# Placing a decoder trunk's matmul operands at 128-byte and 512-byte boundaries of their SBUF partition

## The chip, the core and the metric

One core of a Trainium2 chip runs the whole kernel as one program. The metric is the device time of one execution in microseconds; several executions are timed and their median is given. One more execution runs under the hardware profiler, and all rows below are from that one.

## What is computed

The reference is a two-layer decoder trunk on 256 tokens of width 1024, in float32. Layer 0 is a half-weighted SwiGLU feed-forward, a Mamba-2 mixer and another feed-forward; layer 1 is a feed-forward, sliding-window attention over shared keys and values, and another feed-forward; a norm ends it. Cut to what matters here:

```
swiglu(h) = (silu(h @ w_gate) * (h @ w_up)) @ w_down      # 1024 -> 2816 -> 1024, four times
x = x + 0.5 * swiglu(rmsnorm(x))                          # layer 0, first
x = x + mamba2_mixer(rmsnorm(x))                          # w_in, conv, scan in chunks of 128, w_out
x = x + 0.5 * swiglu(rmsnorm(x))                          # layer 0, second
k, v = shared_kv(x)                                       # one K and one V projection
x = x + 0.5 * swiglu(rmsnorm(x))                          # layer 1, first
x = x + swa_sink_attention(rmsnorm(x), k, v)              # w_q, softmax with sinks, w_o
x = x + 0.5 * swiglu(rmsnorm(x))                          # layer 1, second
return rmsnorm(x)
```

## The kernel before

**Units.** All weights are cut into 341 units of 128 x 1024 numbers, listed in `ORDER`; a unit feeds a product with a contraction of 1024 (gate, up, and the projections) or with 1024 outputs (down, the two output projections). Activations lie transposed: a tile holds 128 features on the partitions and the 256 tokens along the free axis.

**Parts.** To keep float32 accuracy with the fast one-pass type (`F32R`), each number is split in two parts, high and low, and a product takes three of the four combinations: high x high, high x low, low x high. For a weight unit, `Weights.high` (L144, ScalarE) rounds the raw weights to the tile `hi`, and `Weights.low` (L155, VectorE) subtracts to get `lo`; both are 128 x 1024, from pools of six buffers each. The raw weights come by DMA, two units (1 MB) at a time, into four buffers `raw`. `Weights.ahead` keeps the split four units ahead of the matmuls.

**The three ways in which a unit is multiplied**, each with 6144 columns streamed through TensorE per unit:

- `wide` (L359), for gate and up: the moving operand's two parts lie side by side in one tile `xs` (512 columns: `xh`, then `xl`). Per 128-column slice of the unit, `hi` is loaded and all 512 columns streamed, then `lo` is loaded and the first 256 streamed: 16 loads and 16 matmuls. In two of the four feed-forwards (`by_part`, where the layer number differs from the index in the layer) the eight `hi` slices come first, then the eight `lo` slices; in the other two they alternate.
- `unit` (L346), for the mixer's projections `sb`, for `q`, and for the keys `kab`: three matmuls of 256 columns per slice, 24 loads and 24 matmuls. `sb` and `q` take the moving parts from `xs`; `kab` takes them from tiles of its own, `xkh` and `xkl`.
- `rows` (L379), for down (`da`), the mixer's output (`sa`) and the attention's output (`aa`): also 24 loads and 24 matmuls of 256 columns, with moving parts in `hh`/`hl`, `yh`/`yl`, `oh`/`ol`.

TensorE follows `ORDER` by hand: gate, up, and four steps behind, down. Small steps on the other engines are put between units by `Slots`.

**Places.** A tile's address within its partition comes from the order of allocation. Without a request, tiles begin at multiples of 32 bytes. These are the places that the built programs give, as the remainder of the first byte by 128 and by 512. A weight slice is 512 bytes of a partition, a moving part 1024.

| tile | before: mod 128 | before: mod 512 | changed: mod 128 | changed: mod 512 |
|---|---|---|---|---|
| `hi`, `lo` (all six buffers, every slice) | 32 | 160 | 0 | 0 |
| `xs` (gate, up, `sb`, `q`) | 0 | 128 | 0 | 128, 256, 384, 0, 0, 128, 256, 384 |
| `hh` / `hl` (down) | 32 | 160 | 0 | 384 / 0 |
| `yh` / `yl` (mixer's output) | 32 | 416 | 0 | 128 / 256 |
| `oh` / `ol` (attention's output) | 32 | 416 | 0 | 128 / 256 |
| `xkh`, `xkl` (keys, values) | 32 | 160 | 0 | all four multiples of 128 |
| `raw` | 32 | 160 | 32 | 416 |

For the value product (`v`) the parts change roles: `xkh` and `xkl` are loaded and `hi` and `lo` are streamed.

Of the kernel before, what the change touches and what calls it, by code (L numbers as in the profile page):

```python
# [10 lines left out]
F32R = mybir.dt.float32r  # L11
# [5 lines left out]
P = 128  # L17
T = 256
D = 1024
KT = D // P  # L20
NF = 2816 // P
LAG = 4
SLACK = 2

NORM_AT = (1, 0, 0, 0)
SCALE_AT = (0, 0, 1, 0)
# [83 lines left out]
class Weights:  # L110
# [27 lines left out]
    def high(self, half=None):  # L138
        u = self.rounded
        c, i = divmod(u, CH)  # L140
        if not half:
            self.hi = self.parts.tile([P, D], F32R, tag="hi", name=f"hi{u}")
        hi, s = self.hi, self.piece(half)
        self.nc.scalar.activation(hi[:, s], self.chunks[c][:, i, s], AF.Copy)  # L144
        if half != 0:
            self.ready[u] = hi
            self.rounded += 1

    def low(self, half=None):
        u = self.cut  # L150
        c, i = divmod(u, CH)
        if not half:
            self.lo = self.parts.tile([P, D], F32R, tag="lo", name=f"lo{u}")
        hi, lo, s = self.ready.get(u, self.hi), self.lo, self.piece(half)
        self.nc.vector.tensor_tensor(lo[:, s], self.chunks[c][:, i, s], hi[:, s].bitcast(F32), ALU.subtract)  # L155
        if half == 0:
            return
        self.ready[u] = (hi, lo)
        self.cut += 1
        if i == CH - 1 or u == NU - 1:  # L160
            del self.chunks[c]
            self.load()
# [53 lines left out]
class Trunk:  # L216
    def __init__(self, ctx, tc, a):
        self.ctx, self.tc, self.nc, self.a = ctx, tc, tc.nc, a
        nc = self.nc
        self.NPART = 6  # L220
        cp = self.cp = ctx.enter_context(tc.tile_pool(name="const", bufs=1))
        self.wk = ctx.enter_context(tc.tile_pool(name="work", bufs=2))
        raw = ctx.enter_context(tc.tile_pool(name="raw", bufs=RAW))
        parts = ctx.enter_context(tc.tile_pool(name="parts", bufs=self.NPART))
        self.ps = ctx.enter_context(tc.tile_pool(name="ps", bufs=4, space=PSUM))
        self.W = Weights(nc, a["w"], raw, parts)

        self.sm = cp.tile([P, NSM], F32, name="sm")
        self.co = cp.tile([P, NCO], F32, name="co")
        xp = [cp.tile([P, 2, T], F32, name=f"X{k}") for k in range(KT // 2)]  # L230
        self.X = [xp[k // 2][:, k % 2] for k in range(KT)]

        self.xs = [cp.tile([P, 2 * T], F32R, name=f"xs{k}") for k in range(KT)]
        self.xh = [x[:, 0:T] for x in self.xs]
        self.xl = [x[:, T:] for x in self.xs]
        self.ones = cp.tile([P, P], F32, name="ones")
        nc.vector.memset(self.ones, 1.0)
        self.mhalf = cp.tile([P, 2], F32, name="mhalf")
        nc.gpsimd.memset(self.mhalf, -0.5)
        self.eps = cp.tile([P, 1], F32, name="eps")  # L240
        nc.gpsimd.memset(self.eps, EPS)
        warm = cp.tile([P, 1], F32, name="warm")
        nc.scalar.activation(warm, self.ones[:, 0:1], AF.Silu)

        def first(t):
            q, h = nc.sync.dma_start, D // 2
            q(self.norms, a["norms"])
            q(xp[0], a["x"][:, 0:2, :])
            q(t[:, 0, :h], a["w"][0, :, 0, :h])
            q(xp[1], a["x"][:, 2:4, :])  # L250
            q(xp[2], a["x"][:, 4:6, :])
            q(t[:, 0, h:], a["w"][0, :, 0, h:])
            q(xp[3], a["x"][:, 6:8, :])
            for i in range(1, CH):
                q(t[:, i, :], a["w"][0, :, i, :])

        self.norms = cp.tile([P, NNO], F32, name="norms")
        self.W.load(first)
        self.W.load()
        nc.sync.dma_start(self.co, a["const"])  # L260
        self.W.load()
        nc.sync.dma_start(self.sm, a["small"])
        for _ in range(RAW - 3):
            self.W.load()
        self.ident = self.cc("ident")
        self.slots = Slots()
# [207 lines left out]
    def ffn(self, l, i, key, nxt):  # L474
        nc, wk = self.nc, self.fw
        self.stage_norm(key)
        accs = self.accs(f"da_{key}")
        hs = {}

        def evac(f, g, u):  # L480
            hh = wk.tile([P, T], F32R, tag="hh", bufs=LAG + 2, name=f"hh_{key}_{f}")
            hl = wk.tile([P, T], F32R, tag="hl", bufs=LAG + 2, name=f"hl_{key}_{f}")
            hs[f] = (hh, hl)

            def e0():
                nc.vector.tensor_tensor(g, g, self.rs, ALU.mult)
                nc.scalar.activation(g, g, AF.Silu)
                nc.vector.tensor_tensor(u, u, self.rs, ALU.mult)

            def e1():  # L490
                nc.vector.tensor_tensor(u, u, g, ALU.mult)
                nc.scalar.activation(hh, u, AF.Copy)

            def e2():
                nc.vector.tensor_tensor(hl, u, hh.bitcast(F32), ALU.subtract)

            wait = max(0, 4 - f) if key == "f0" else 2 if f == 0 else 0
            self.slots.chain(wait, [e0, e1, e2])

        def product(name, f, t):  # L500

            b = self.bank(f"{name}_{key}_{f}")
            if self.W.pos == 0:
                self.slots.at(0, lambda: nc.scalar.copy(t, b[:, 0:T]))
                self.unit((name, l, i, f), b[:, 0:T])
                return

            def add():
                nc.scalar.copy(t, b[:, T:])  # L509
                nc.vector.tensor_tensor(t, b[:, 0:T], t, ALU.add)  # L510

            self.slots.at(0, add)
            self.wide((name, l, i, f), b, by_part=l != i and f > 0)

        for f in range(NF):
            g, u = (wk.tile([P, T], F32, tag=n, bufs=4, name=f"{n}s_{key}_{f}") for n in "gu")
            product("g", f, g)
            evac_now = lambda: evac(f, g, u)
            self.slots.late(0, evac_now)
            product("u", f, u)  # L520
            if l == 1 and i == 0 and f == 0:
                self.split_k()
            if l == 1 and i == 0 and f == 5:
                self.shared_k()
            if f >= LAG:
                self.down(l, i, f - LAG, hs, accs)
        for f in range(NF - LAG, NF - 2):
            self.down(l, i, f, hs, accs)
        self.tail([(("d", l, i, f), *hs.pop(f)) for f in (NF - 2, NF - 1)], accs, nxt)
# [15 lines left out]
    def ssm(self, nxt):  # L545
        nc, tc, wk, sl = self.nc, self.tc, self.sw, self.slots
# [17 lines left out]
        B, C, xs, zs, CSB, CB, xdt, ys, M = ({} for _ in range(9))  # L564
        yh, yl, sq, R = {}, {}, {}, {}
# [188 lines left out]
        def ysplit(tt):  # L754
            y = ys[tt]
            w = self.s("snw", tt)
            h = yh[tt] = wk.tile([P, T], F32R, tag="yh", bufs=6, name=f"yh{tt}")
            l = yl[tt] = wk.tile([P, T], F32R, tag="yl", bufs=6, name=f"yl{tt}")
            sl.at(0, lambda: A.activation(h, y, AF.Copy, scale=w))
            sl.at(1, lambda: V.scalar_tensor_tensor(l, y, w, h.bitcast(F32), ALU.mult, ALU.subtract))  # L760

# [58 lines left out]
        for what in seq[:-2]:  # L820
            if what[0] == "so":
                tt = what[1]
# [39 lines left out]

    def split_k(self):
        wk = self.kp
        self.xkh = [wk.tile([P, T], F32R, name=f"xkh{k}") for k in range(KT)]
        self.xkl = [wk.tile([P, T], F32R, name=f"xkl{k}") for k in range(KT)]
        for k in range(KT):
            w = self.nw("kvn", k)
            self.slots.at(2 + k, lambda k=k, w=w: self.nc.scalar.activation(self.xkh[k], self.X[k], AF.Copy, scale=w))
            self.slots.at(  # L870
                3 + k,
                lambda k=k, w=w: self.nc.vector.scalar_tensor_tensor(
                    self.xkl[k], self.X[k], w, self.xkh[k].bitcast(F32), ALU.mult, ALU.subtract
                ),
            )
# [26 lines left out]
    def att(self, nxt):  # L902
        nc, wk, sl = self.nc, self.aw, self.slots
        V, A = nc.vector, nc.scalar
        self.stage_norm("att")
        Q, S, SM_, PT, oh, ol = ({} for _ in range(6))
# [94 lines left out]
        def pv(j):  # L1001
# [8 lines left out]
                nc.tensor.matmul(o[:, P:T], self.V[:, 1, v], p[:, 2], start=False, stop=True, skip_group_check=True)  # L1010
            for r in range(2):
                o = bs[r * (not one)][:, r * one * T : r * one * T + T]
                h = oh[j, r] = wk.tile([P, T], F32R, tag="oh", bufs=4, name=f"oh{j}_{r}")
                ol[j, r] = wk.tile([P, T], F32R, tag="ol", bufs=4, name=f"ol{j}_{r}")
                A.activation(h, o, AF.Copy)
            for r in range(2):
                o = bs[r * (not one)][:, r * one * T : r * one * T + T]
# [214 lines left out]
```

## Time and profile before

| | us |
|---|---|
| median of 3 runs (1061.9 to 1063.26) | 1062.36 |
| the profiled execution | 1063.96 |
| its span, from the first to the last instruction | 1062.2 |
| TensorE busy (matmuls) | 1040.4 |
| VectorE busy | 775.3 |
| ScalarE busy | 627.5 |

The profiled execution's own time is 1.8 us over its span, and 1.6 us over the median. Matmuls overlap in TensorE's pipeline, so the "mean ns of one" of a matmul (283 ns for 256 columns) is not what it costs; the distance from one matmul's start to the next is. The chain of waits gives that distance: it merges a unit's matmuls in one piece, with the time until the next piece starts.

### The profile page before, as it was taken

Reading aid. Unit: us, or ns where it says so; the run is one execution under the profiler, and the core shown is the slowest. Engines: PE = TensorE matmul, PEld = TensorE weight load, DVE = VectorE, ACT = ScalarE, POOL = GpSimd, SP = SyncE. Lnnn points to the kernel's source line nnn. Section 1 sums busy time; section 2 is a strip of 40 time slices with the busy share of each in tenths; the row PEclk is TensorE's granted clock in tenths of the full one; section 3 lists DMA queues with packets and bytes.
Section 4 is the critical chain, followed back from the end, with each engine's and each line's share of the span. In section 5 each row is a group of like instructions: output and inputs, shape, how many; then the busy total and the mean of one; then the engine's idle time right before and its main releaser. Section 6 shows DMA issues by size and latency. Waiting matters only on the chain.

```text
span 1062.2 us, 18342 instructions
## 1 busy us (share of the span) xinstructions
PE 1040.4 (98%) x7290; PEld 961.3 (90%) x7290; DVE 775.3 (73%) x1420; ACT 627.5 (59%) x1106; POOL 79.5 (7%) x122
## 2 busy tenths in 40 slices
PE   8999999999999999999999999999999999999996
PEld 7899999999989898999999899999998898999996
DVE  4866666788999967766667796666689777666664
ACT  6555555579886756555555664555565765555554
POOL 3000000210111112000000200000022020000000
PEclk9999999999999999999999999999999999999998
DMA  8555455447545454545555465455544334545521
GB/s 303 202 186 198 165 197 185 174 176 273 182 149 211 160 180 165 193 168 196 188 192 189 148 216 187 170 194 192 197 170 160 110 145 173 198 172 193 191 100 40
DMA packets 30132, 190.84 MB, mean 180 GB/s; under 512 B 3904, under 2 KB 5728, under 8 KB 8544
## 3 DMA queue, kind: packets, MB, share of 16 engines
q1 hardware_dynamic: 30048, 189.69, 50.0%
q8 instruction: 57, 0.93, 0.4%
q14 instruction: 27, 0.22, 0.1%
HBM read 187.27 MB, written 1.10 MB: 177 GB/s over the span
## 4 chain that ended last, share of the span: by engine, by line
PE 81%; DVE 10%; ACT 4%; DMA 2%; POOL 1%; issue 1%; SPq 0%; ACTq 0%; DVEq 0%; POOLq 0%
PE da_f L379 23%; PE u_f L359 23%; PE g_f L359 22%; PE sa L379 4%; PE sb L346 3%; DVE lo L155 2%; PE aa L379 2%; PE q L346 1%; DMA csb<-cs_scratch 1%; DVE xs L598 1%; DVE xs L391 1%; ACT hi L144 1%; DVE E L720 1%; ACT E L715 1%; DMA raw<-w 1%
## 5 line engine op out<-in xcount | busy, mean ns | idle before, releaser
L155 DVE TENSOR_TENSOR lo<-raw,hi 128x1024 fp32r<-128x1024 f32 (+1 forms) x343 | 415.0, 1213 | 15.8 <-ACT hi L144 15.6
L144 ACT ACTIVATE hi<-raw 128x1024 fp32r<-128x1024 f32 (+1 forms) x343 | 357.4, 1047 | 22.3 <-PE da_f L379 6.2
L359 PE MATMUL u_f<-xs,hi 128*128 128x512 f32 x704 | 218.6, 398 | 0.0
L359 PE MATMUL g_f<-xs,hi 128*128 128x512 f32 x696 | 214.7, 397 | 0.6 <-DVE xs L391 0.4
L379 PE MATMUL da_f<-hh_f,hi 128*128 128x256 f32 x704 | 199.1, 283 | 0.0
L379 PE MATMUL da_f<-hl_f,hi 128*128 128x256 f32 x704 | 199.1, 283 | 0.0
L379 PE MATMUL da_f<-hh_f,lo 128*128 128x256 f32 x704 | 198.9, 283 | 0.0
L359 PEld LDWEIGHTS u_f<-xs,hi 128*128 128x128 f32 x704 | 129.8, 188 | 27.9
L359 PEld LDWEIGHTS g_f<-xs,hi 128*128 128x128 f32 x696 | 128.2, 189 | 27.4 <-DVE xs L391 1.5
L359 PE MATMUL u_f<-xs,lo 128*128 128x256 f32 x704 | 150.2, 281 | 0.0
L359 PE MATMUL g_f<-xs,lo 128*128 128x256 f32 x696 | 147.8, 281 | 0.0
L379 PEld LDWEIGHTS da_f<-hh_f,hi 128*128 128x128 f32 x704 | 134.5, 191 | 1.6
L379 PEld LDWEIGHTS da_f<-hh_f,lo 128*128 128x128 f32 x704 | 134.9, 192 | 0.0
L379 PEld LDWEIGHTS da_f<-hl_f,hi 128*128 128x128 f32 x704 | 134.8, 192 | 0.0
L510 DVE TENSOR_TENSOR gs_f<-g_f,gs_f 128x256 f32<-128x256 f32 x87 | 36.9, 424 | 121.9 <-ACT gs_f L509 121.9
L359 PEld LDWEIGHTS u_f<-xs,lo 128*128 128x128 f32 x704 | 116.0, 189 | 3.9
L359 PEld LDWEIGHTS g_f<-xs,lo 128*128 128x128 f32 x696 | 114.3, 189 | 3.8
L346 PE MATMUL sb<-xs,hi 128*128 128x256 f32 x656 | 107.8, 284 | 0.0
L510 DVE TENSOR_TENSOR us_f<-u_f,us_f 128x256 f32<-128x256 f32 x88 | 37.3, 423 | 91.1 <-ACT us_f L509 91.0
L509 ACT COPY us_f<-u_f 128x256 f32<-128x256 f32 x88 | 32.6, 371 | 113.1 <-PE u_f L359 113.1
L346 PEld LDWEIGHTS sb<-xs,hi 128*128 128x128 f32 x656 | 93.4, 188 | 1.1 <-issue 0.5
L509 ACT COPY gs_f<-g_f 128x256 f32<-128x256 f32 x87 | 32.1, 369 | 97.3 <-PE g_f L359 97.3
(252 smaller groups left out, 1376.7 us busy)
## 6 DMA issues: line engine op xcount, KB each, us to landing
raw<-w SPq DMA_DIRECT2D x168, 1024.0 KB, 4.9
csb<-cs_scratch SPq DMA_DIRECT2D x8, 768.0 KB, 7.0
raw<-w SPq DMA_DIRECT2D x4, 512.0 KB, 7.9
X<-x SPq DMA_DIRECT2D x4, 256.0 KB, 5.7
Q<-r_q SPq DMA_DIRECT2D x32, 32.0 KB, 1.9
out<-o SPq DMA_DIRECT2D x3, 256.0 KB, 2.2
ca<-const_att SPq DMA_DIRECT2D x1, 704.0 KB, 4.1
raw<-w SPq DMA_DIRECT2D x2, 256.0 KB, 5.7
```

The lines of the kernel that those rows point to most:

```text
L144: self.nc.scalar.activation(hi[:, s], self.chunks[c][:, i, s], AF.Copy)
L155: self.nc.vector.tensor_tensor(lo[:, s], self.chunks[c][:, i, s], hi[:, s].bitcast(F32), ALU.subtract)
L346: nc.tensor.matmul(out, w[:, k * P : (k + 1) * P], x[k], start=n == 0, stop=n == len(passes) - 1)
L359: self.nc.tensor.matmul(out[:, 0:c], w[:, k * P : (k + 1) * P], x[k], start=n == 0, stop=n == len(passes) - 1, skip_group_check=True,)
L379: nc.tensor.matmul(out, w[:, s], x, start=f and j < 4 and m == 0, stop=e and m == 2, skip_group_check=True)
L391: nc.vector.scalar_tensor_tensor(self.xl[j], self.X[j], wcol(j), self.xh[j].bitcast(F32), ALU.mult, ALU.subtract)
L509: nc.scalar.copy(t, b[:, T:])
L510: nc.vector.tensor_tensor(t, b[:, 0:T], t, ALU.add)
L598: V.scalar_tensor_tensor(out, u[:, tap : tap + T], self.s("convw", tap * 24 + c), out, ALU.mult, ALU.add)
L715: A.activation(e, e, AF.Exp, scale=-1.0)
L720: V.tensor_tensor(f, f, c, ALU.mult)
```

## The change

Eleven tile allocations get a wish for alignment: the two weight parts at multiples of 512 bytes, all moving parts at multiples of 128. Nothing else is edited. On every engine the instructions, their operands, their order and their waits are the same; only addresses differ, those of tiles that were allocated later too.

```diff
+BLOCK = 128
...
-            self.hi = self.parts.tile([P, D], F32R, tag="hi", name=f"hi{u}")
+            self.hi = self.parts.tile([P, D], F32R, align_bytes=4 * BLOCK, tag="hi", name=f"hi{u}")
...
-            self.lo = self.parts.tile([P, D], F32R, tag="lo", name=f"lo{u}")
+            self.lo = self.parts.tile([P, D], F32R, align_bytes=4 * BLOCK, tag="lo", name=f"lo{u}")
...
-        self.xs = [cp.tile([P, 2 * T], F32R, name=f"xs{k}") for k in range(KT)]
+        self.xs = [cp.tile([P, 2 * T], F32R, align_bytes=BLOCK, name=f"xs{k}") for k in range(KT)]
...
-            hh = wk.tile([P, T], F32R, tag="hh", bufs=LAG + 2, name=f"hh_{key}_{f}")
-            hl = wk.tile([P, T], F32R, tag="hl", bufs=LAG + 2, name=f"hl_{key}_{f}")
+            hh = wk.tile([P, T], F32R, align_bytes=BLOCK, tag="hh", bufs=LAG + 2, name=f"hh_{key}_{f}")
+            hl = wk.tile([P, T], F32R, align_bytes=BLOCK, tag="hl", bufs=LAG + 2, name=f"hl_{key}_{f}")
...
-        self.xkh = [wk.tile([P, T], F32R, name=f"xkh{k}") for k in range(KT)]
-        self.xkl = [wk.tile([P, T], F32R, name=f"xkl{k}") for k in range(KT)]
+        self.xkh = [wk.tile([P, T], F32R, align_bytes=BLOCK, name=f"xkh{k}") for k in range(KT)]
+        self.xkl = [wk.tile([P, T], F32R, align_bytes=BLOCK, name=f"xkl{k}") for k in range(KT)]
```

The tiles `yh`, `yl`, `oh` and `ol` get `align_bytes=BLOCK` in the same way.

## Rows read from the trace of the kernel before

**Rows 1.** The page, busy time by engine, and TensorE's granted clock in 40 slices.
```profile
PE 1040.4 (98%) x7290; PEld 961.3 (90%) x7290; DVE 775.3 (73%) x1420; ACT 627.5 (59%) x1106; POOL 79.5 (7%) x122
...
PEclk9999999999999999999999999999999999999998
```

**Rows 2.** Busy time by stage: four feed-forwards (1st, 4th, 5th, 7th), mixer (2nd, 3rd), attention (6th).
```profile
core 0: us, PE busy (x) PEld busy (x) DVE busy (x) ACT busy (x) POOL busy (x), PEclk, DMA share, GB/s
28.40:201.94 173.54, 173.54 (x1153) 159.29 (x1152) 121.12 (x201) 94.96 (x156) 2.41 (x3) 1.00 0.53 189
205.99:343.05 137.06, 133.76 (x1126) 129.45 (x1125) 122.68 (x241) 104.64 (x188) 17.30 (x29) 1.00 0.55 201
350.35:401.20 50.85, 50.24 (x411) 48.94 (x410) 40.44 (x70) 30.99 (x54) 7.43 (x10) 0.97 0.48 166
405.37:593.24 187.87, 187.71 (x1236) 171.68 (x1235) 129.86 (x217) 103.50 (x170) 7.22 (x11) 1.00 0.52 185
594.17:784.49 190.32, 190.32 (x1267) 174.94 (x1267) 134.76 (x227) 105.15 (x174) 7.30 (x11) 1.00 0.54 190
788.55:860.89 72.34, 70.56 (x587) 64.37 (x587) 61.58 (x181) 45.28 (x123) 13.96 (x16) 1.00 0.42 147
865.18:1050.34 185.16, 185.16 (x1219) 169.41 (x1219) 122.74 (x208) 97.36 (x157) 2.39 (x5) 1.00 0.44 157
```

**Rows 3.** Chain of waits, first feed-forward, `hi` and `lo` alternating: start, us, matmuls.
```profile
91.21 2.83 PE u_f L359 x16
94.04 2.87 PE da_f L379 x24
96.92 2.83 PE g_f L359 x16
```

**Rows 4.** Chain of waits, second feed-forward, by part.
```profile
434.25 2.81 PE g_f L359 x16
437.06 2.81 PE u_f L359 x16
439.87 2.87 PE da_f L379 x24
```

**Rows 5.** Chain of waits: projections of `unit`, two units each.
```profile
212.35 5.68 PE sb L346 x48
...
628.62 5.75 PE kab L346 x48
```

**Rows 6.** TensorE's matmuls in order of time, in down: start, us of one.
```profile
432.40 0.28 PE L379 MATMUL da_f<-hl_f,hi 128*128 128x256 f32 x1
432.52 0.28 PE L379 MATMUL da_f<-hh_f,lo 128*128 128x256 f32 x1
432.64 0.28 PE L379 MATMUL da_f<-hh_f,hi 128*128 128x256 f32 x1
```

**Rows 7.** The same view in the mixer's output, before and after the clock rises.
```profile
351.13 0.41 PE L379 MATMUL sa<-yl,hi 128*128 128x256 f32 x1
...
352.63 0.41 PE L379 MATMUL sa<-yh,hi 128*128 128x256 f32 x1
...
353.28 0.28 PE L379 MATMUL sa<-yh,lo 128*128 128x256 f32 x1
...
354.48 0.28 PE L379 MATMUL sa<-yl,hi 128*128 128x256 f32 x1
```

**Rows 8.** Busy time by stage (columns as in rows 2), for the two stretches of rows 7.
```profile
351.13:352.63 1.50, 1.50 (x9) 1.50 (x8) 1.50 (x3) 1.50 (x4) 0.00 (x0) 0.50 0.00 0
353.28:354.48 1.20, 1.20 (x13) 1.20 (x11) 1.20 (x4) 1.18 (x2) 0.00 (x0) 1.00 0.75 171
```

**Rows 9.** The page, costliest groups: the splits' mean times.
```profile
L155 DVE TENSOR_TENSOR lo<-raw,hi 128x1024 fp32r<-128x1024 f32 (+1 forms) x343 | 415.0, 1213 | 15.8 <-ACT hi L144 15.6
L144 ACT ACTIVATE hi<-raw 128x1024 fp32r<-128x1024 f32 (+1 forms) x343 | 357.4, 1047 | 22.3 <-PE da_f L379 6.2
```

More of the change, by code (lines that the diff above doesn't have):

```diff
@@ L756, in ysplit @@
             w = self.s("snw", tt)
-            h = yh[tt] = wk.tile([P, T], F32R, tag="yh", bufs=6, name=f"yh{tt}")
-            l = yl[tt] = wk.tile([P, T], F32R, tag="yl", bufs=6, name=f"yl{tt}")
+            h = yh[tt] = wk.tile([P, T], F32R, align_bytes=BLOCK, tag="yh", bufs=6, name=f"yh{tt}")
+            l = yl[tt] = wk.tile([P, T], F32R, align_bytes=BLOCK, tag="yl", bufs=6, name=f"yl{tt}")
             sl.at(0, lambda: A.activation(h, y, AF.Copy, scale=w))
@@ L1012, in pv @@
                 o = bs[r * (not one)][:, r * one * T : r * one * T + T]
-                h = oh[j, r] = wk.tile([P, T], F32R, tag="oh", bufs=4, name=f"oh{j}_{r}")
-                ol[j, r] = wk.tile([P, T], F32R, tag="ol", bufs=4, name=f"ol{j}_{r}")
+                h = oh[j, r] = wk.tile([P, T], F32R, align_bytes=BLOCK, tag="oh", bufs=4, name=f"oh{j}_{r}")
+                ol[j, r] = wk.tile([P, T], F32R, align_bytes=BLOCK, tag="ol", bufs=4, name=f"ol{j}_{r}")
                 A.activation(h, o, AF.Copy)
```

## The prediction

> **What bounds the kernel now.** I read the page first, then the stages, then the chain of waits, then single starts. The page has TensorE busy for 98% of the span, with 90% or more of the full clock granted in all slices but the last [rows 1]; the reader is to see that no other engine is near that. By stage, TensorE is busy in each of the four feed-forwards for the whole stretch but 0.2 us; VectorE stands at 65 to 71%, ScalarE at 53 to 56% there [rows 2]. These four stretches are 173.5 + 187.9 + 190.3 + 185.2 = 736.9 us of the 1062.2, so the time is set by how fast matmuls follow each other, not by a wait. In the mixer's first part TensorE is idle for 3.3 us of 137.1, but VectorE is busy for 90% of it, so there a gain on TensorE can be eaten [rows 2].
>
> The chain of waits gives the pace of a unit. Each unit streams 6144 columns, whatever its form. In the first feed-forward gate and up take 2.83 us and down 2.87 [rows 3]; in the second 2.81 and 2.87 [rows 4]. In down the starts lie 0.12 us apart, for 256 columns [rows 6]. What would it be without loss? Rows 7 show it: in the mixer's output the same matmuls first start 0.214 us apart (1.50 us for 7), then 0.120 (1.20 us for 10). The granted clock was half in the first stretch (1.2 GHz; TensorE had waited just before) and full in the second (2.4 GHz), after 2 us of matmuls on end [rows 8]. 0.214 us at 1.2 GHz is one column per clock, 213.3 ns, nothing lost; at 2.4 GHz that would be 106.7 ns, and 13.3 ns (32 columns' time) are lost per matmul. So at the full clock something besides the array limits the stream, and what is left to read faster is the operands. A unit without loss is 6144 / 2.4 GHz = 2.56 us; the loss is 0.27 us for gate or up where the parts alternate, 0.25 by part, 0.31 in down.
>
> **The change part by part.** No instruction is added, removed or moved, and no wait: the order on each engine, the DMA queue of SP included, is the same, and the changed program differs in addresses alone. So every term is a change in what one instruction takes.
>
> *Moving operands from 32 to 0 past a multiple of 128.* The trace of before holds a comparison of just this. `sb` and `kab` are the same function and line, with the same weights at 32; `sb` moves `xs` (at 0), `kab` moves `xkh` and `xkl` (at 32). Two units of `sb` take 5.68 us, two of `kab` 5.75 [rows 5]: 0.035 us a unit, and `kab` has the pace of down (2.875 against 2.87 [rows 4]). Units whose moving parts get to 0 are 88 of down, 16 of the mixer's output, 8 of the attention's, 2 of keys and 2 of values, 116 in all: 116 x 0.035 = 4.1 us. The 88 of down lie on the path with no wait beside them [rows 2 to 4]; that is 3.1 us of it.
>
> *Weights from 32 to 0 past a multiple of 128, and of 512.* No row shows a weight at 0. An end above: all loss goes. That is 88 x 0.27 + 88 x 0.25 for gate and up, 88 x 0.31 for down, and in the other 77 units at most 0.28 each: 23.8 + 22.0 + 27.3 + 21.6 = 94.7 us, of which 4.1 is counted already. An end below: rows where weights and moving parts stand at the same place (both at 32: down, `kab`) lose 13.3 ns for each of the 24 matmuls, every time, while rows where they differ lose less on average (`sb`: 5.68 / 48 = 118.3 ns). If sameness costs, gate, up, `sb` and `q` get there too: `sb` and `q`, 49 units, 0.035 more each, 1.7 us; gate and up, if each 256 columns take 0.12, 2.88 a unit, 88 x (0.05 + 0.07) = 10.6 us. Together 12.3 us slower, and the 4.1 are not gained.
>
> Between these ends, 90.6 us faster and 16.4 slower than the first term alone, the nearest rows are those of `sb` and gate, which have one of the two operands in place already; they say no more is lost or won than now: 0. A second reading of the same rows comes out close to it: one step of 13.3 ns lost per weight load where both operands stand alike. Gate and up have 16 loads, so 2.56 + 16 x 0.0133 = 2.773 us a unit, and gain 88 x 0.057 + 88 x 0.037 = 8.3 us; `sb` and `q` lose 1.7, down stays: 6.6 us faster. I forecast between the two readings, **5 us faster**.
>
> *The splits.* `lo` (1213 ns) and `hi` (1047 ns) now write to aligned tiles and read `raw` at 32 as before [rows 9]. No row shows them with another placement. In the feed-forwards three of each per 8.5 us are 3.6 and 3.1 us; the cover is TensorE's 8.5 us there, with VectorE idle for some 30% of it, 2.5 us [rows 2]; `lo` would have to take 0.8 us longer each to use that up. In the mixer's first part the cover is thin: 41 units x 1.2 us = 49 us of `lo`; 5% either way is 2.5 us. I take 0 and keep 2.5 for the range. The DMAs land in `raw` at another remainder by 512 and the same by 128; 189 GB/s in the stage [rows 2] is covered by four buffers: 0.
>
> *The sum.* The profiled execution took 1063.96 us (span 1062.2 and 1.8 around it). Less 5 it is 1059.0. It stands 1.6 us over the median of the runs, so the median is expected at 1062.36 - 5 = 1057.4, say **1057 us**.
>
> **The rivals.**
>
> *The loss goes away, wholly or for a good part.* For it: down's 120.0 ns is what nine pieces of 128 bytes take at 13.3 ns each, and 1024 bytes that begin at 32 touch nine such pieces, at 0 eight. A weight slice of 512 bytes touches five now and four then. Read so, gate and up lose because the weights are out of place, and with both in place nothing is left to lose. Against it: `sb` already has its moving parts at eight pieces and gains only 1.7 ns of 13.3. Wholly it would give 1062 - 95 = 967 us; some of that would turn into waits for VectorE in the mixer (90% busy there), and I take half of the feed-forwards' loss as the centre: 1062 - 37 = 1025, with 985 to 1045 as its span. The Trainium skill, page "TensorE: Matmul & The Clock Gate", section "Back-to-back issue gap", has a gap of columns / 2.4 GHz + 2.5 ns at the full clock. By it a unit of gate would take 8 x (215.8 + 109.2) = 2.60 us, where rows 3 and 4 show 2.83 and 2.81; if placement is what this trace has in the way, an estimate from that page is 88 x (0.23 + 0.21 + 0.22), 58 us less in the feed-forwards alone, near 1004.
>
> *Sameness costs (slower).* TensorE reads weights and moving parts at once; if both step through the same 128-byte pieces in step, one must wait for the other, once per 256 columns. Place: gate and up, 176 units, and `sb` and `q`. Price: the 12.3 us above, 1062.4 + 12.3 = 1074.7. It decides from the point at which a unit of gate takes more than 2.83 and 2.81. For it: all rows at one place show exactly 24 losses for 24 matmuls, at remainders of 160 and of 416 by 512 alike [rows 6, 7]. Against it: the same 24 are told as well by nine pieces for eight.
>
> *Nothing happens.* The placement by 32 is already enough, and `kab` is slower than `sb` for another reason (its 24 matmuls follow in another order than the first eight of `sb`, or the row of 5.68 is short by its edges, 0.07 us on one pair of units). Then 1062.4 us. The Trainium skill, page "SBUF — State Buffer", section "Specifications (TRN2)", gives lines of 16 bytes; by that rule a start at 32 is a start of a line, and the change would do nothing. Rows 5 do not bear this out, by 0.07 us.
>
> **How the numbers follow.** About 0.2% (2 us) is what a measurement of this kernel can tell from no change. Forecast, by either of its readings (1055 to 1060): 0.42. The loss goes for a good part: 0.29. Sameness costs: 0.17. Nothing: 0.12. Faster is the first two, 0.71; same 0.12; slower 0.17. For a range that leaves 2 in 10 out, I go down to 1005, which leaves out the part of the second case that loses nearly nothing (about 0.1), and up to 1069, which takes in half of the slower case and the 2.5 us of the splits. The forecast's own range is 1053 to 1061.
>
> **What would show it.** Down's pieces in the chain at 2.84 instead of 2.87, or starts in down under 0.12 apart, show the first term right; at 2.87 still, it is wrong and sameness or nothing is right. Gate and up at 2.77 show the second reading; at 2.81 to 2.83, the first; under 2.7, the loss goes; near 2.88, sameness costs. Means of `lo` and `hi` off 1213 and 1047 would show that placement works on the splits. The prediction is wrong if the four feed-forwards, now 736.9 us together, come out above 737 or below 722.

## The result, and the profile after

The changed kernel takes 1053.66 us in the median (1052.27 to 1054.58, 4 runs), the kernel before 1062.81 beside it: a ratio of 0.9913, 95% interval 0.9896 to 0.9931. That is 9.15 us faster (7.3 to 11.1 by the interval); 5 were forecast. The profiled execution took 1053.63 us, its span is 1051.9.

The page of the changed kernel, to be held against [rows 1, 9]: TensorE is busy 10.1 us less, the other engines as long as before, and `lo` and `hi` take what they took (1213 and 1047 ns before), so the aligned tiles do nothing for the splits.

```profile
PE 1030.3 (98%) x7290; PEld 955.1 (91%) x7290; DVE 775.3 (74%) x1420; ACT 627.9 (60%) x1106; POOL 79.3 (8%) x122
...
L157 DVE TENSOR_TENSOR lo<-raw,hi 128x1024 fp32r<-128x1024 f32 (+1 forms) x343 | 415.6, 1215 | 15.7 <-ACT hi L146 15.5
L146 ACT ACTIVATE hi<-raw 128x1024 fp32r<-128x1024 f32 (+1 forms) x343 | 357.3, 1047 | 21.0 <-PE da_f L381 6.1
```

Busy time by stage, cut at the same instructions as in [rows 2]: the stretch, its length behind the colon pair (with TensorE's busy time), then the other engines.

```profile
28.39:199.90 171.51, 171.51 (x1153) 158.26 (x1152) 121.21 (x201) 94.98 (x156) 2.41 (x4) 1.00 0.53 191
203.93:340.95 137.02, 133.87 (x1125) 129.52 (x1125) 123.06 (x241) 104.88 (x188) 17.30 (x29) 1.00 0.55 201
347.62:397.15 49.53, 48.94 (x411) 47.69 (x410) 40.69 (x70) 31.34 (x55) 7.43 (x11) 1.00 0.48 171
401.31:587.18 185.87, 185.69 (x1235) 170.55 (x1235) 129.84 (x217) 103.68 (x170) 7.19 (x11) 1.00 0.53 187
588.11:776.43 188.32, 188.32 (x1267) 173.79 (x1267) 134.61 (x227) 105.29 (x174) 7.31 (x11) 1.00 0.55 192
780.47:852.75 72.28, 70.48 (x588) 64.27 (x588) 61.58 (x181) 45.32 (x123) 13.93 (x16) 1.00 0.43 147
857.02:1040.01 182.99, 182.99 (x1220) 168.25 (x1220) 122.84 (x208) 97.38 (x157) 2.39 (x5) 1.00 0.45 158
```

The feed-forwards lose 2.0, 2.0, 2.0 and 2.2 us, 8.2 together. The mixer's projections (second row) and the attention gain nothing. The mixer's output is 1.3 us shorter; in the kernel before it had a stretch at half clock [rows 7, 8], here the clock is full. The unit in that stretch took 4.25 us from its start to the next unit's and takes 3.05 here, so 1.2 of the 1.3 us are the clock's. That is not the change's doing: down_at_0 below, which has all of the change but the place of `hh`, takes 4.56 us for this unit, at a granted clock of 0.53.

The chain of waits shows the pace of a unit, against [rows 3 to 5]: first feed-forward, second, then two units each of `sb` and `kab`.

```profile
93.19 2.85 PE da_f L381 x24
96.04 2.78 PE g_f L361 x16
98.82 2.79 PE u_f L361 x16
...
210.31 5.68 PE sb L348 x48
...
435.39 2.85 PE da_f L381 x24
438.24 2.78 PE g_f L361 x16
441.02 2.77 PE u_f L361 x16
...
622.18 5.68 PE kab L348 x48
```

Gate and up fall from 2.83 (first feed-forward) and 2.81 (second) to between 2.77 and 2.79; down from 2.87 to 2.85; `sb` stays at 5.68, `kab` gets there from 5.75. So about three quarters of the gain are in gate and up: 44 x (0.046 + 0.040) + 44 x (0.029 + 0.040) = 6.8 us, and 72 units of down that follow up give 72 x 0.023 = 1.7.

For differences of 0.01 us a unit is measured from the start of its first matmul to the start of the next unit's first. This table has the median over a run's units, in ns, without the units that hold a wait; each is a whole unit of 6144 columns (2560 without loss; 2880 is a loss of 13.3 ns for each of 24 matmuls). Pairs are gate, up. "Distance" is the weights' place less that of the moving part, by 256 bytes (the remainder); the reason for the 256 is in the experiments. "Down after up" is the 72 units that follow another form, "down after down" the 16 at the feed-forwards' ends. Some medians stand between two paces that take turns: in the alternating feed-forwards of dist0 and dist256 gate takes 2814 and 2832, up 2819 and 2831, down 2875 and 2882; in those of moving_only gate takes 2803 and 2817, up 2811 and 2820, down 2873 and 2883; in those of weights_only up takes 2806 and 2814, down 2864 and 2876. `sb` in the changed kernel runs from 2818 to 2847.

| kernel | distance for gate, up, `sb` | gate, up alternating | gate, up by part | distance for down | down after up | down after down | `sb` after `sb` |
|---|---|---|---|---|---|---|---|
| before | 32 | 2826, 2827 | 2813, 2813 | 0 | 2874 | 2880 | 2840 |
| changed | 0 and 128 | 2780, 2787 | 2784, 2773 | 128 (`hh`), 0 (`hl`) | 2851 | 2880 | 2840 |
| shift96 | 128 | 2794, 2814 | 2800, 2800 | 0 | 2872 | 2880 | 2847 |
| all_at_32 | 128 | 2794, 2814 | 2800, 2799 | 0 | 2868 | 2880 | 2848 |
| moving_only | 32 and 160 | 2813, 2814 | 2808, 2803 | 160 | 2877 | 2880 | 2840 |
| weights_only | 128 | 2804, 2806 | 2815, 2799 | 160 | 2866 | 2880 | 2847 |
| dist0 | 0 | 2822, 2820 | 2793, 2793 | 0 | 2880 | 2880 | 2880 |
| dist256 | 0 | 2815, 2820 | 2793, 2793 | 0 | 2880 | 2880 | 2880 |
| spread_w256 | 0 and 128 | 2780, 2787 | 2784, 2773 | 128, 0 | 2851 | 2880 | 2840 |
| down_at_0 | 0 and 128 | 2780, 2787 | 2797, 2773 | 0 | 2871 | 2880 | 2840 |
| down_at_128 | 0 and 128 | 2778, 2787 | 2802, 2773 | 128 | 2848 | 2847 | 2840 |
| xs_step32 | all eight multiples of 32 | 2800, 2812 | 2821, 2820 | 128, 0 | 2845 | 2880 | 2854 |

### The profile page after: what moved, and what is told of

Its sections match the earlier page's. It is cut to its first block, busy times and chain, and to the rows that moved or that the text cites. A ratio compares the mean times of both kernels' runs of the same rounds, so it can differ in the third digit from the quotient of the medians.

```text
span 1051.9 us, 18342 instructions
## 1 busy us (share of the span) xinstructions
PE 1030.3 (98%) x7290; PEld 955.1 (91%) x7290; DVE 775.3 (74%) x1420; ACT 627.9 (60%) x1106; POOL 79.3 (8%) x122
## 4 chain that ended last, share of the span: by engine, by line
PE 81%; DVE 10%; ACT 4%; DMA 2%; POOL 1%; issue 1%; SPq 0%; ACTq 0%; DVEq 0%; POOLq 0%
PE da_f L381 23%; PE u_f L361 23%; PE g_f L361 22%; PE sa L381 3%; PE sb L348 3%; DVE lo L157 2%; PE aa L381 2%; PE q L348 1%; DVE xs L600 1%; DMA csb<-cs_scratch 1%; DVE xs L393 1%; ACT hi L146 1%; DMA raw<-w 1%; DVE E L722 1%; ACT E L717 1%
## 5 line engine op out<-in xcount | busy, mean ns | idle before, releaser
L146 ACT ACTIVATE hi<-raw 128x1024 fp32r<-128x1024 f32 (+1 forms) x343 | 357.3, 1047 | 21.0 <-PE da_f L381 6.1
L361 PE MATMUL u_f<-xs,hi 128*128 128x512 f32 x704 | 215.4, 394 | 0.0
L361 PE MATMUL g_f<-xs,hi 128*128 128x512 f32 x696 | 211.7, 393 | 0.6 <-DVE xs L393 0.6
```

The lines of the kernel that those rows point to most:

```text
L361: self.nc.tensor.matmul(out[:, 0:c], w[:, k * P : (k + 1) * P], x[k], start=n == 0, stop=n == len(passes) - 1, skip_group_check=True,)
```

## The experiments

**Is it the place, or the distance?** Four kernels take the change apart. In shift96 unused bytes move all later tiles of the kernel before, so that weights and moving parts stand at multiples of 128, but the weights not at multiples of 512:

```diff
         self.norms = cp.tile([P, NNO], F32, name="norms")
+        cp.tile([P, 24], F32, name="padb")
```

> The kernel before with 96 unused bytes ahead of the raw weights, which puts all weights and all moving parts at 0 past a multiple of 128 bytes, but the weights at 256 past a multiple of 512 and all xs at 128. Theory 'place by 128': as the changed kernel, 1053.7 us within 1.5, gate and up 2.77 to 2.79 us, down after up 2.85. Rival 'the 512 matters': a weight slice then lies across a multiple of 512, and gate and up keep a part of their loss, 2.80 or more, over 1056 us.

In all_at_32 nothing at all stands at a multiple of 128, but everything at the same place:

```diff
+        cp.tile([P, 8], F32, name="pada")
         self.xs = [cp.tile([P, 2 * T], F32R, name=f"xs{k}") for k in range(KT)]
...
         self.norms = cp.tile([P, NNO], F32, name="norms")
+        cp.tile([P, 24], F32, name="padb")
```

> The kernel before with 32 unused bytes ahead of xs and 96 behind, so that xs too stands at 32, as weights and all other moving parts do. 'Only the distance counts': gate and up get the 2.77 to 2.79 of the changed kernel, down stays at 2.87: 1055 us. 'Pieces of 128 bytes': 2048 bytes of xs now touch 17 pieces instead of 16 and the weights five as before: gate and up no faster than before, 2.83 or more, 1062 us or slower.

shift96: 1058.51 us, ratio 0.9968 (0.9956 to 0.9979). all_at_32: 1059.24 us, 0.9971 (0.9959 to 0.9982). The chain of waits, first shift96, then all_at_32, with pieces of the first and the second feed-forward:

```profile
98.19 2.79 PE g_f L360 x16
100.98 2.81 PE u_f L360 x16
...
435.87 2.80 PE u_f L360 x16
...
441.53 2.80 PE g_f L360 x16
```

```profile
96.45 2.79 PE g_f L361 x16
99.25 2.81 PE u_f L361 x16
...
434.23 2.80 PE u_f L361 x16
...
439.89 2.80 PE g_f L361 x16
```

The two give the same paces, and gate and up agree to 1 ns (table), though one has everything at 0 past a multiple of 128 and the other at 32. What they share is every distance: weights less `xs` is 58,496 bytes in both. So the place alone counts for nothing here, and the theory of pieces of 128 bytes, which wanted all_at_32 no faster than before, falls. But both missed the 2.77 to 2.79 that the theories had for them: they have little over a third of the change's gain (3.4 and 3.1 us by their ratios), so something beyond the distance by 128 is in it.

The other two take the edits apart. moving_only is the changed kernel without the alignment of `hi` and `lo`, weights_only the changed kernel with that alone. The first cut, against the changed kernel; `lo` in the same way:

```diff
-            self.hi = self.parts.tile([P, D], F32R, align_bytes=4 * BLOCK, tag="hi", name=f"hi{u}")
+            self.hi = self.parts.tile([P, D], F32R, tag="hi", name=f"hi{u}")
...
```

> The changed kernel without the alignment of hi and lo: weights at 32, all moving parts at 0. Both 'pieces of 128 bytes' and 'only the distance between weights and moving parts counts': gate and up as before (2.81 and 2.83), down at the 2.84 of sb, 1059 us. If the weights' place does all the work: 1062.4, down at 2.87.

The second, against the changed kernel; all other moving parts in the same way:

```diff
-        self.xs = [cp.tile([P, 2 * T], F32R, align_bytes=BLOCK, name=f"xs{k}") for k in range(KT)]
+        self.xs = [cp.tile([P, 2 * T], F32R, name=f"xs{k}") for k in range(KT)]
...
```

> The changed kernel with the alignment of hi and lo alone: weights at 0, xs at 0, the other moving parts at 96. 'Pieces of 128 bytes': gate and up as in the changed kernel (2.77 to 2.79), down keeps its nine pieces, 2.87 or more: 1055.5 us or more. 'Only the distance counts': moving less weights is then the same in down as in sb before (96 by 128), so down takes 2.84: 1052 to 1054.

moving_only: 1061.21 us, 0.9986 (0.9975 to 0.9998); weights_only: 1060.33 us, 0.9983 (0.9974 to 0.9991). The chain of moving_only, then of weights_only:

```profile
435.32 2.80 PE u_f L361 x16
438.12 2.88 PE da_f L381 x24
```

```profile
436.46 2.86 PE da_f L381 x24
439.32 2.82 PE g_f L361 x16
442.14 2.80 PE u_f L361 x16
```

Both theories had down at 2.84 in moving_only; it is at 2.88, slower than before by a hair. Down gains nothing from the place of its moving parts, and in weights_only next to nothing (2866 for 2874, where 2840 was expected) from having `sb`'s old distance by 128: it stands at 160 by 256, `sb` before at 32. The two halves of the change are worth 1.5 and 1.8 us by their ratios, 3.3 together, where the whole is worth 9.2: what does the work is in both together. Where the halves differ from the whole is that moving_only has `xs` in different places from tile to tile but a distance that is no multiple of 128, and weights_only the reverse. That `xs` tiles get different places was no aim of the edit: with a wish for alignment the tiles mostly lie 2176 bytes apart in the built program instead of 2048.

shift96 and weights_only have the same distance for gate and up and yet differ by up to 15 ns. In the last two rounds of gate and up ahead of a feed-forward's first unit of down they agree to 1 ns (by part, gate 2820 and 2821, up 2800 and 2799). The difference comes in with down, which stands at 0 in one and at 160 in the other: what ran before a unit counts too.

**The mean of the distances, or the mix?** Two kernels hold the distance at 0 and at 256 by 512 in all slices, with 120 and 56 in the place of shift96's 24; a third keeps the mix and moves the weights off the multiple of 512.

```diff
+        cp.tile([P, 120], F32, name="padb")
```

> The kernel before with 480 unused bytes ahead of the raw weights: weights and xs both at 128 past a multiple of 512, so their distance is 0 by 512 in all eight slices (128 in shift96, 384 in weights_only; the changed kernel has 0, 128, 256 and 384, twice each). Theory 'mean of the distances': 128 gave 2.802 us a unit of gate or up, 384 gave 2.806, the changed kernel's mix 2.781, so distances 0 and 256 must give 2.758 on average. Rival 'the mix itself': 2.80 here as at the other single distances, 1058 us.

> The same with 224 unused bytes: distance 256 by 512 in all slices. 'Mean of the distances': with dist0 2.758 us a unit on average. 'The mix itself': 2.80, 1058 us.

```diff
-            self.hi = self.parts.tile([P, D], F32R, align_bytes=4 * BLOCK, tag="hi", name=f"hi{u}")
+            self.hi = self.parts.tile([P, D], F32R, align_bytes=BLOCK, tag="hi", name=f"hi{u}")
... (lo in the same way)
+        cp.tile([P, 64], F32, name="padb")
```

> The changed kernel with all weights at 256 past a multiple of 512 (alignment of hi and lo 128, 256 unused bytes ahead), xs over all four places by 512 as in the changed kernel. 'Distances alone count': they are the same four in another order, so gate and up 2.77 to 2.79 and 1053.7 us within 2. Rival 'weights at multiples of 512': 2.80 or more, 1057 us or more.

dist0: 1060.59 us, 0.9981 (0.9972 to 0.9989). dist256: 1061.02 us, 0.9984 (0.9975 to 0.9993). spread_w256: 1053.57 us, 0.9912 (0.9897 to 0.9928). The chains of dist0, its last piece from the last feed-forward, and of spread_w256:

```profile
97.08 2.83 PE g_f L360 x16
99.91 2.82 PE u_f L360 x16
...
212.58 5.74 PE sb L347 x48
...
433.40 2.79 PE g_f L360 x16
436.19 2.79 PE u_f L360 x16
438.99 2.88 PE da_f L380 x24
...
883.35 2.77 PE g_f L360 x16
886.12 2.77 PE u_f L360 x16
888.90 2.87 PE da_f L380 x24
891.76 2.83 PE g_f L360 x16
```

```profile
95.82 2.78 PE g_f L362 x16
98.60 2.79 PE u_f L362 x16
...
434.72 2.85 PE da_f L382 x24
437.57 2.78 PE g_f L362 x16
440.35 2.77 PE u_f L362 x16
```

spread_w256 repeats the changed kernel's paces: the multiple of 512 is not needed. dist0 and dist256 are alike too, by part to the nanosecond, so only the distance by 256 shows. Over a whole feed-forward no single distance comes near the mix: 0 gives medians of 2793 to 2822, 128 gives 2794 to 2815, where the mean of the distances wanted 2758 from the zeros. So it is the mix of 0 and 128 over the `xs` tiles (in order 128, 0, 128, 0, 0, 128, 0, 128) that gains in gate and up, and no single one of its distances. It does not help everywhere: `sb` takes 2840 with the mix as with the single distance 32, and down, with `hh` at 128 and `hl` at 0, takes 2880 after down, as at 0. And dist0 shows what sameness costs: `sb` goes to the full 2880, 5.74 in the chain, 40 ns over before.

One stretch does not fit a pace that goes by distance alone. In the last feed-forward of dist0 and of dist256, gate and up that follow each other ahead of the first unit of down take 2772 to 2775, the best that the mix reaches; from the first unit of down on, they take turns between 2814 and 2832, 2819 and 2831 as told above. In the first feed-forward, with the same order and distances, they take 2819 to 2831 ahead of down too. So at distance 0 units of the same form and order have two paces, and what chooses between them was not found.

**Is one step lost per load?** In lo_wide the lo slices too are multiplied by all 512 columns; it adds the low x low product, so it does more work.

```diff
-        passes = [(k, w, x, n) for k in range(KT) for w, x, n in ((hi, self.xs, 2 * T), (lo, self.xh, T))]
+        passes = [(k, w, x, n) for k in range(KT) for w, x, n in ((hi, self.xs, 2 * T), (lo, self.xs, 2 * T))]
```

> The changed kernel with the lo slices of gate and up multiplied by all 512 columns of xs (the low x low product is added too): 16 loads and 16 matmuls of 512 columns per unit, 8192 / 2.4 GHz = 3.413 us without loss. 'One step of 13.3 ns per load': 3.413 + 16 x 0.0133 = 3.63 us a unit. 'Loss by streamed columns', at the changed kernel's 0.22 us per 6144: 3.413 + 0.295 = 3.71 us. 176 units are 0.85 or 0.93 us longer each: about 1203 or 1217 us.

One run: 1208.77 us. From its chain, the first and the second feed-forward:

```profile
96.22 3.71 PE u_f L361 x16
...
451.09 3.67 PE g_f L361 x16
```

The loss over 3.413 is 0.26 to 0.30 us for 16 loads, 19 to 22 steps of 13.3 ns. It grows with the columns but less than in proportion. Neither rule holds: it is not one step per load.

**Down.** down_at_0 and down_at_128 place `hh` and `hl` alike, at distance 0 and at 128 from the weights:

```diff
-            hh = wk.tile([P, T], F32R, align_bytes=BLOCK, tag="hh", bufs=LAG + 2, name=f"hh_{key}_{f}")
+            hh = wk.tile([P, T], F32R, align_bytes=4 * BLOCK, tag="hh", bufs=LAG + 2, name=f"hh_{key}_{f}")
... (hl in the same way)
```

> The changed kernel with hh and hl at multiples of 512, as the weights: their distance from the weights is then 0 by 256, as in the kernel before (in the changed kernel it is 128 for hh and 0 for hl). Theory 'down gains by the place of hh': down after up goes back from 2.851 to 2.874, gate and up stay at 2.78: 1055.5 us. Rival 'down gains by the state in which gate and up leave TensorE's reads': down after up stays near 2.85, 1053.7 us.

```diff
-            hh = wk.tile([P, T], F32R, align_bytes=BLOCK, tag="hh", bufs=LAG + 2, name=f"hh_{key}_{f}")
+            hh = wk.tile([P, T + 32], F32R, align_bytes=4 * BLOCK, tag="hh", bufs=LAG + 2, name=f"hh_{key}_{f}")[:, 32:]
... (hl in the same way)
```

> The changed kernel with hh and hl both at 128 past a multiple of 512, so both at distance 128 by 256 from the weights, as xs was in shift96, where sb took 2.847. 'Distance 0 is what costs down its full step per matmul': down after up 2.84, down after down 2.847 instead of 2.88, 1052.3 us. Rival 'a moving tile that is streamed again and again costs a step each time, wherever it lies': down after down stays at 2.88, 1053.7 us within 1.

down_at_0: 1055.19 us, 0.9929 (0.9916 to 0.9943). down_at_128: 1054.07 us, 0.9916 (0.9903 to 0.993). The chain of down_at_128, a by-part feed-forward and the five units of down that end the first one; the last line is those five in the changed kernel:

```profile
185.55 14.24 PE da_f L381 x120
...
435.82 2.85 PE da_f L381 x24
438.66 2.80 PE g_f L361 x16
441.46 2.77 PE u_f L361 x16
```

```profile
185.81 14.37 PE da_f L381 x120
```

Both expectations for down came in: at 0 it goes back to 2871, near the 2874 of before, and at 128 down after down leaves the 2880 that it had in every kernel so far, for 2847, the value of `sb` at that distance. But gate by part goes from 2784 to 2802 where it follows down, and gives most of it back: 34 x 18 ns = 0.6 us lost, against 0.8 gained in down (summed over its 88 units). The time as a whole missed its 1052.3 us: 1054.07 cannot be told from the changed kernel's. A unit's pace hangs on the unit before it.

**Does any mix do?** In xs_step32 the `xs` tiles lie 2080 bytes apart:

```diff
-        self.xs = [cp.tile([P, 2 * T], F32R, align_bytes=BLOCK, name=f"xs{k}") for k in range(KT)]
+        self.xs = [cp.tile([P, 2 * T + 8], F32R, name=f"xs{k}") for k in range(KT)]
...
+        self.xs = [x[:, : 2 * T] for x in self.xs]
```

> The changed kernel with the eight xs tiles 2080 bytes apart, so that their places by 256 are 128, 160, 192, 224, 0, 32, 64, 96: mixed, but only two of them at a multiple of 128. 'Any mix helps': gate and up 2.77 to 2.79 and 1053.7 us within 1.5. Rival 'the mix must be of multiples of 128': 2.80 or more, 1057 us or more (moving_only, mixed at 32 and 160, had 2.803 to 2.814).

1059.88 us, 0.9977 (0.9968 to 0.9986). Its chain:

```profile
433.68 2.82 PE u_f L362 x16
436.50 2.88 PE da_f L382 x24
439.38 2.82 PE g_f L362 x16
```

Not any mix: by part it is slower than before. Of the three mixes tried, 0 and 128, 32 and 160 (moving_only), and all multiples of 32, only the first gains much.

**A version to beat both.** out_at_128 gives `yh`, `yl`, `oh`, `ol` the distance 128, and `hh`, `hl` too where gate does not give it back:

```diff
+            if l == i:
+                wk.tile([P, 32], F32, tag="padh", bufs=1, name=f"padh_{key}_{f}")
             hl = ...
...
+            wk.tile([P, 32], F32, tag="pady", bufs=1, name=f"pady{tt}")
             l = yl[tt] = ...
... (ol in the same way)
```

> The changed kernel with 128 unused bytes ahead of yl and ol, and ahead of hl in the two feed-forwards whose parts alternate, so that yh, yl, oh, ol and there hh and hl all stand at distance 128 by 256 from the weights. 'Distance 0 costs the full step': the units of sa and aa that follow one another go from 2.88 to 2.847, as down did in down_at_128; the first and the last feed-forward take 0.25 us less each as there, the other two what they take in the changed kernel: 0.5 + up to 24 x 0.033 = 1.3 us under the changed kernel, 1052.4 us. Rival 'a later loss gives it back' (as gate by part did in down_at_128): 1053.7 us within 0.5.

1053.76 us, 0.992 (0.9906 to 0.9933): the time of the changed kernel. Its chain has the units of the mixer's output:

```profile
359.24 5.90 PE sa L381 x48
366.64 5.89 PE sa L381 x48
377.59 15.68 PE sa L381 x132
```

Against 5.95, 5.91 and 15.82 in the changed kernel. The units did what was expected (2847 for 2880, and 0.24 us less in the first and the last feed-forward), some 0.7 us in all of the 1.3 expected, which is less than the runs of one kernel differ by. It does not beat the changed kernel by anything that can be measured.

## Why the prediction was right, and where it was not

**What bounds it** held: nothing but TensorE's pace changed, and the feed-forwards passed the gain on whole, 8.2 us, to 728.7 together, between the 722 and 737 that were to bear it out. The splits, put at 0, took what they took. Whether VectorE, 90% busy in the mixer's projections, would have eaten a gain there was not tried: `sb` kept its pace.

**Direction and range** held, at 9.15 us faster for a forecast of 5, and 1053.66 us lies in the forecast's own 1053 to 1061. In good part that was luck: of the two terms that make the time, one was counted for a cause that is not there and gave less than half of its price, and the one that gave most was put at nothing.

**The first term failed**: moving operands from 32 to 0, 116 x 0.035 = 4.1 us. It took `sb` against `kab` as a test of the moving parts' place. The two rows differ in that, but also in the distance from the weights, 32 against 0, and it is this that the runs bear out: `sb` at distance 0 (dist0) takes `kab`'s 2880, and all_at_32 shows that the place alone does nothing. moving_only gave down nothing (2877 for 2874). What down did gain in the changed kernel, 0.023 a unit, comes from `hh` standing 128 away from the weights (down_at_0 takes it back): 1.7 us where the term had 3.1 for down. The sign given for it, down at 2.84 or at 2.87 still, came out between the two, at 2.85.

**The second term was mis-sized**: the weights' place was put at 0 for gate and up, by the nearest rows. These gained 0.029 to 0.046 us a unit, 6.8 us, three quarters of the result, through the mix of distances; that the `xs` tiles get different distances stood in the table of places, and no term asked what that does.

**The second reading** had gate and up at 2.773 and 6.6 us in all, the nearest to the result, and its sign, gate and up at 2.77, came in; but by a rule that does not stand: where both operands stand alike in every slice (dist0), gate and up take 2793 by part and 2814 to 2832 alternating, and 2773 only in the one short stretch of the last feed-forward, and lo_wide loses more than a step per load. It had `sb` and `q` slower by 0.035, which is right at distance 0 (dist0) and wrong for the changed kernel, whose mix leaves `sb` at 2840.

**The rivals.** *The loss goes away* did not happen: in gate and up 0.21 to 0.23 of 0.25 to 0.27 us are still lost. *Sameness costs* is true as a mechanism for `sb` (2880 at distance 0), but gate and up, where its price lay, never came to 2880, and the change does not bring sameness: it spreads the distances. *Nothing happens*, with the 16-byte lines that the Trainium skill gives ("SBUF — State Buffer", "Specifications (TRN2)") as its reason, is refuted by 9.15 us: a start at 32 is no worse in itself, but distances of 0, 32 and 128 between two operands give 2880, 2840 and 2847 for the same `sb`. The gap of the Trainium skill's page "TensorE: Matmul & The Clock Gate" ("Back-to-back issue gap"), 2.60 us for a unit of gate, is not reached by any of the placements tried; the best median is 2.773. The page gives that formula for a single matmul by itself, not for a stream of loads and matmuls as here. The estimate's 0.22 us for a unit of down should be 0.25 (2.87 less 24 x 109.2 ns), which makes its 58 us 61.

**Left open.** Why two streams at certain distances cost each other time, why the cost comes in steps of 13.3 ns (6.7 in some units), and why a mix of 0 and 128 is better than either, was not shown; that two reads of TensorE meet is an argument, not a reading. The runs show that the pace goes by the distance, by 256 bytes, by the form of the product, and by what ran before (at distance 0, gate and up have two paces). For the `xs` tiles, single distances other than 0, 32 and 128 were not tried, nor mixes over the weights instead of the moving parts.

## What to carry to other kernels

Where matmuls of 4-byte operands follow each other at the full clock and cost a constant share over columns / clock (here 8 to 12%), with no wait in the chain, vary the addresses: it costs no instruction, and here gave 0.9%. Vary the distance between the weights and the moving part, not each one's alignment, and measure each form by itself: equal places were the worst case for `sb` and down, but better than 32 for gate and up by part (2793 for 2813); moving parts that differ by 128 bytes among the tiles were the best for gate and up. A change to one form moves the next one too. A comparison of two rows is a test of one cause only if they differ in nothing else; look for what comes along.

## What was not expected of the hardware

In most stretches the pace of a unit repeats to the nanosecond, while VectorE, ScalarE and the DMAs work beside it: 37 of 40 units of up by part at 2813 in the kernel before, and the same 2780, 2787, 2784 and 2773 in the changed kernel and in spread_w256. The distances do not always settle it: at distance 0 it was 2773 in one stretch and 2819 to 2831 in another of the same form and order. At half clock none of it is seen: 0.214 us for 256 columns at distance 0, one column per clock [rows 7, 8], where the full clock has 0.120 for the 0.107 of one column per clock.
